# Second-half gates and two RG-LRU tiles moved ahead of the heads, five pairs of projection columns by seven block products

## The chip, the cores and the metric

The kernel runs on one core of one Trainium2 chip. The time is the device time of one execution in microseconds (us). Lower is better. TensorE (PE) does the matrix products, VectorE (DVE) and ScalarE (ACT) the elementwise work, GpSimd (POOL) a few copies, and the queue of SyncE (SP) issues nearly all transfers between HBM and the on-chip memory.

## The reference, cut to what matters

One layer of a hybrid decoder for 2048 prompt tokens and 8 sample rows, width 1024. Cut to the parts that the change touches:

```python
hn = _rmsnorm(x, g_norm) * (1.0 + scale[:, None]) + shift[:, None]
z = hn @ w_in                                  # 1024 x 5136
xa, za, q, k, v, glr, zg = jnp.split(z, SPLITS, axis=-1)
xc = conv_b + sum(xp[:, j:j + T] * conv_w[j] for j in range(CONV_W))
gx, ga = sigmoid(blockdiag(xc, w_gate_x)), sigmoid(blockdiag(xc, w_gate_a))
_, h = lax.associative_scan(_lin_comb, (a, u), axis=1)     # RG-LRU, a and u from gx, ga, xc
y_lru = h * silu(za)
o, S_new = _gla_chunked(qh, kh, vh, log_alpha, S0)         # 4 heads
y_gla = rmsnorm_per_head(o) * silu(zg)
mix = concat([y_lru, y_gla]) @ w_out                       # 2048 x 1024
x = x + gate[:, None] * mix                                # then a final RMSNorm
```

## The kernel before, in words

Every float32 product is made of three products of rounded parts: a matrix is split into a high part (a rounding copy on ACT) and a low part (a subtraction on DVE), and high*high, high*low and low*high are added in one PSUM bank. `hh` and `hl` are the two parts of the normalized input `hn` for 1024 tokens, transposed: eight blocks of 128 rows (`kt`) by 1024 tokens, with 8 more columns for the samples.

The tokens are worked off in two halves. The first half has 1024 tokens in two segments of 512. The second half has 1024 tokens and the 8 samples, 1032 columns in segments of 384, 384 and 264 (`SEGS`). `project` (L636 on, matmuls L642 to L644) makes one column tile of 128 output features for one segment: 24 matmuls.

In each half the loop over `HEADS` calls `gla_head`, then `lru`. A head computes its values (`values`, L327 to L329), q and k, its decay, and two tiles of its gate `zg` (`silu2`, L1031 and L1032); the chunked attention of 128 tokens at a time (`chunks`) is put between these units. `lru` does one to three of the eight RG-LRU tiles: `xa_unit` (projection, convolution, block-diagonal gates, scan at L1199) and `za_unit`. Tiles 6 and 7 of the second half are done after all heads, while the last part is prepared. The last part, the output projection (class `Pair`, matmuls at L1483), already uses seven block products in place of eight.

Order is set by hand with a clock. `after(u, f)` puts `f` into a heap with the due time clock + u, and `tick` moves the clock on by 1 for each projected segment, by 0.5 for each of the eight token tiles of `values`, and calls what is due. A call made during a tick counts its own `after` from the clock of that tick, so a chain with steps of 0.5 moves by one link per projected segment. The compiler's scheduler may then still reorder instructions that don't depend on each other; `behind(q)` pins an instruction behind the last one written so far on its engine.

One such chain is `out_weights`. It prepares the weights of the output projection in 16 steps `s`: 0 to 7 for one half of the output columns, 8 to 15 for the other; within each eight, four steps for the weights `wd[0]`, needed first, then four for `wd[1]`. A step loads `r` (L745, two transfers of 256 KB), multiplies it by the gate (two L766, 512 wide), makes four sums (L766, 256 wide), in the `wd[1]` steps also splits two of them (L770 and L771), stores seven or five blocks of 128 KB (L784), two more from the splits (L775), and loads the next `r`. The pool `hp`, which holds all this, has one buffer for `r`. A step has four links of 0.5 (six in a `wd[1]` step), then 0.5 and 1 up to the stores, 1 up to the next load, 1.5 up to the next first link. A pause (`phase`) holds the chain during the change of halves.

After the second half the pools `gp` (the heads) and `hp` are closed, and the pool `mp` is laid over their memory (`reuse_waits="tile"`: a tile of the new pool waits until the old tiles under it are done with). `load_w(0, 0, 0)` (L1347) then loads the first weights of the output projection into it, and `split_w` splits them (L1333 and L1336).

Of the kernel before, what the change touches and what calls it, by code (L numbers as in the profile page):

```python
# [34 lines left out]
SEGS = (((0, 512), (512, 512)), ((0, 384), (384, 384), (768, 264)))  # L35
HEADS = (3, 0, 1, 2)
LRU_TILES = ((0,), (1, 2), (3, 4), (5, 6, 7))

# [11 lines left out]
def hybrid_kernel(ctx, tc, i, o):  # L50
# [21 lines left out]

# [107 lines left out]
    def modulate(xt, g, kts):  # L180

        c = slice(g * 256, (g + 1) * 256)
        for k2 in range(kts[0], kts[1], 2):
            pt = tps().rearrange("p (k t) -> p k t", k=2)
            f = xp.tile([P, 2, 256], F32, tag="f512", name="hnf")
# [47 lines left out]
    def hn_load(g, now=True):  # L233

        xt = []
        for j in range(2):
            q = 2 * g + j
            if q in (0, 1, 7):
                x = xp.tile([P, TH + NS], F32, tag="xt", name="xt")[:, :D]
            elif q == 2:  # L240
                x = gp.tile([P, D], F32, tag="on", name="xo")
            else:
                x = gp.tile([P, D], F32, tag="vh" if q < 5 else "vl", name="xv", bufs=2)
# [386 lines left out]
    def open_lp():  # L630
# [3 lines left out]
        hp = hpx.enter_context(tc.tile_pool(name="hp", bufs=1, reuse_waits="tile"))  # L634
# [35 lines left out]
    def after(units, fn, gla=False):  # L670
        clock[1] += 1
        heapq.heappush(pend, (clock[0] + units, clock[1], fn, gla))
# [17 lines left out]
    def ada_gate():  # L690
# [3 lines left out]
        def step(kt):  # L694
# [4 lines left out]
            def mm():  # L699
# [6 lines left out]
                else:  # L706
# [3 lines left out]
                    after(4, out_weights)  # L710
# [5 lines left out]
    phase = [0]  # L716

    def out_weights():


        def begin(q):
# [5 lines left out]
            r = load(8 * q)  # L727

            def add():
                with behind(V):  # L730
                    V.tensor_tensor(g, g, bt, op=OP.add)
                after(0.5, lambda: step(8 * q, r, g))
# [15 lines left out]
        def one(ops, end):  # L748


            if phase[0] == 1:
                after(0.5, lambda: one(ops, end))
                return
# [5 lines left out]
        def step(s, r, g):  # L759
# [19 lines left out]
            def store():  # L779
# [19 lines left out]
        begin(0)  # L799
# [43 lines left out]
    def new_values():  # L843
        return [[gp.tile([P, 4, DV], F32R, tag=tag, name=tag, bufs=2) for _ in range(2)] for tag in ("vh", "vl")]
# [181 lines left out]

    def silu2(w, c0, n):

        ps = project(w, c0, n)
        z = lp.tile([P, 512], F32, tag="zs", name="zs", bufs=4)[:, :n]  # L1030
        S.activation(z, ps, AF.Tanh, scale=0.5)  # L1031
        V.scalar_tensor_tensor(z, z, 1.0, ps, op0=OP.add, op1=OP.mult)  # L1032
# [16 lines left out]
    def gla_head(half, h, wv=None):  # L1049
# [8 lines left out]
        prep, zs, os_, state, wz = {}, {}, [None], [], []  # L1058

        def chunks(s, c):  # L1060

            nch = min(SEGS[half][s][1], TH - SEGS[half][s][0]) // P
            if c == 0:
                prep[s, "run"] = gla_start(half, h, s, prep[s])
                after(1.5 if half else 1, lambda: chunks(s, 1), True)
                return
            gla_chunk(half, h, s, c - 1, prep[s], prep[s, "run"], v)
            if c < nch:
                after(1, lambda: chunks(s, c + 1), True)
                return  # L1070
            gla_norm(nch, prep[s, "run"])
            after(2.5 if half else 1 if s + 1 < ns else 2, lambda: finish(s), True)
# [823 lines left out]
```

## Time and profile before

| what | value |
|---|---|
| median of 3 runs | 1453.5 us (1451.63 to 1454.32) |
| span of the profiled execution | 1451.9 us |
| PE busy | 1429.6 us, 98% of the span |
| DVE busy | 993.1 us, 68% |
| ACT busy | 670.7 us, 46% |
| moved | 268.53 MB, mean 185 GB/s |
| granted TensorE clock | 0.998 |

The page gives the execution's own time as its span. The median of the runs is 1.6 us above it. A busy PE is not a PE at its peak, since a matmul's time in the trace includes its way through the pipeline: the 128x512 matmuls of the output projection are 390 ns long in the table of groups and start 227 ns apart. So the distance between starts is what a matmul costs.

By its lines, the trace falls into a start (to about 70 us), the first half (to about 570 us), the second half (to about 1072 us, when the last gate unit of tile 5 ends), tiles 6 and 7 (to about 1127 us) and the output projection.

### The profile page before, as it was taken

The page shows a single profiled execution, that of the slowest core. Times are in us where ns is not written, and L with a number is a line of the kernel's source. Part 1 is how long each engine was busy: PE and PEld are TensorE (multiplying, and loading weights), DVE is VectorE, ACT ScalarE, POOL GpSimd, SP SyncE. Part 2 cuts the span into 40 slices and gives each one's busy share as a digit, 9 for nine tenths or more (in the row PEclk, how much of TensorE's full clock was granted, in tenths as well). Part 3 has the DMA queues.
Part 4 walks back from the last instruction along what each step waited for, and adds up shares of the span by engine and source line. Part 5 has one row for each costly group of instructions (what it writes and reads, how often), then busy time and mean ns, then how long its engine had stood idle before and what let it go on. Part 6 is the DMA issues. An engine that isn't in the chain of part 4 may idle for free.

```text
span 1451.9 us, 23133 instructions
## 1 busy us (share of the span) xinstructions
PE 1429.6 (98%) x8753; PEld 1269.0 (87%) x8753; DVE 993.1 (68%) x2390; ACT 670.7 (46%) x1214; POOL 28.4 (2%) x44
## 2 busy tenths in 40 slices
PE   7999999999999999999999999999999999999998
PEld 6888888888898888999999999999998887788886
DVE  5756555765765778567567656576678976688886
ACT  4643533652545477534533643446267522144332
POOL 1200000000000002000000000000000000000000
PEclk9999999999999999999999999999999999999999
DMA  9755554645555664335645544564552767694452
GB/s 333 263 178 174 186 170 146 202 147 174 182 174 192 204 212 163 95 130 177 210 138 165 178 141 162 180 200 135 179 197 90 282 226 270 231 355 140 137 168 113
DMA packets 173605, 268.53 MB, mean 185 GB/s; under 512 B 10482, under 2 KB 126866, under 8 KB 171053
## 3 DMA queue, kind: packets, MB, share of 16 engines
q1 hardware_dynamic: 141093, 250.00, 50.9%
q10 hardware_dynamic: 32048, 16.00, 3.7%
q8 instruction: 69, 1.13, 0.3%
q0 software_dynamic: 352, 1.05, 0.2%
q14 instruction: 43, 0.35, 0.1%
HBM read 168.55 MB, written 98.52 MB: 184 GB/s over the span
## 4 chain that ended last, share of the span: by engine, by line
PE 52%; issue 34%; DVE 5%; ACT 4%; DMA 4%; SPq 1%; POOL 0%; ACTq 0%; DVEq 0%; POOLq 0%
PE acc L1483 12%; PE tp L1483 9%; PE acc L642 6%; PE acc L643 6%; PE acc L644 6%; PE acc L327 2%; PE acc L328 2%; PE acc L329 2%; DMA wada<-in_w_ada_dram 1%; DMA w<-parts 1%; PE po L976 1%; DVE cv L1145 1%; PE pss L1691 1%; ACT L881 1%; PE tp L942 0%
## 5 line engine op out<-in xcount | busy, mean ns | idle before, releaser
L642 PE MATMUL acc<-hh,w 128*128 128x384 f32 (+2 forms) x1256 | 446.2, 355 | 3.6 <-DMA w<-parts 3.3
L643 PE MATMUL acc<-hl,w 128*128 128x384 f32 (+2 forms) x1256 | 434.9, 346 | 0.0
L644 PE MATMUL acc<-hh,w 128*128 128x384 f32 (+2 forms) x1256 | 434.0, 346 | 0.0
L642 PEld LDWEIGHTS acc<-hh,w 128*128 128x128 f32 x1256 | 235.9, 188 | 26.2 <-DVE xb L899 3.6
L643 PEld LDWEIGHTS acc<-hl,w 128*128 128x128 f32 x1256 | 236.1, 188 | 19.4 <-issue 0.4
L644 PEld LDWEIGHTS acc<-hh,w 128*128 128x128 f32 x1256 | 235.9, 188 | 19.5
L1483 PE MATMUL acc<-w,a 128*128 128x512 f32 (+1 forms) x792 | 184.8, 386 | 0.0
L1483 PEld LDWEIGHTS acc<-w,a 128*128 128x128 f32 x792 | 146.8, 188 | 33.2 <-issue 3.4
L327 PE MATMUL acc<-w,hh 128*128 128x256 f32 (+1 forms) x508 | 145.5, 286 | 0.0
L329 PE MATMUL acc<-w,hl 128*128 128x256 f32 (+1 forms) x508 | 143.3, 282 | 0.2 <-DVE hl L216 0.2
L328 PE MATMUL acc<-w,hh 128*128 128x256 f32 (+1 forms) x508 | 143.1, 282 | 0.0
L1483 PE MATMUL tp<-w,a 128*128 128x512 f32 x564 | 136.0, 391 | 0.0
L1483 PEld LDWEIGHTS tp<-w,a 128*128 128x128 f32 x564 | 105.2, 188 | 26.8 <-issue 5.2
L1031 ACT ACTIVATE zs<-acc 128x512 f32<-128x512 f32 (+2 forms) x80 | 41.0, 513 | 177.3 <-PE acc L644 177.1
L1032 DVE SCALAR_TENSOR_TENSOR zs<-zs,acc 128x512 f32<-128x512 f32 (+2 forms) x80 | 46.2, 578 | 86.0 <-ACT zs L1031 81.4
L327 PEld LDWEIGHTS acc<-w,hh 128*128 128x128 f32 x508 | 96.0, 189 | 1.6 <-DVE vl L860 0.4
L329 PEld LDWEIGHTS acc<-w,hl 128*128 128x128 f32 x508 | 96.0, 189 | 0.4 <-DVE hl L216 0.4
L328 PEld LDWEIGHTS acc<-w,hh 128*128 128x128 f32 x508 | 95.5, 188 | 0.2
L1333 ACT CAST a<-s 128x512 fp32r<-128x512 f32 x61 | 36.5, 619 | 95.3 <-issue 35.9
L1145 DVE SCALAR_TENSOR_TENSOR cv<-xa,vecT,cv 128x512 f32<-128x512 f32 (+2 forms) x120 | 75.9, 640 | 1.8 <-ACT cv L1143 1.4
L158 ACT ACTIVATE junk<-on 128x256 bf16<-128x256 f32 x64 | 26.6, 416 | 78.0 <-DVE on L981 69.6
L859 ACT CAST vh<-acc 128x256 fp32r<-128x256 f32 x56 | 20.7, 370 | 90.0 <-PE acc L329 71.7
(343 smaller groups left out, 2234.6 us busy)
## 6 DMA issues: line engine op xcount, KB each, us to landing
w<-parts SPq DMA_DIRECT2D x38, 1024.0 KB
parts<-w SPq DMA_DIRECT2D x37, 1024.0 KB
wr<-in_w_in_dram SPq DMA_DIRECT2D x44, 512.0 KB
a<-mixd SPq DMA_DIRECT2D x63, 256.0 KB
w<-wd SPq DMA_DIRECT2D x12, 1024.0 KB
wada<-in_w_ada_dram SPq DMA_DIRECT2D x16, 512.0 KB
r<-in_w_out_dram SPq DMA_DIRECT2D x32, 256.0 KB
mixd<-zs ACTq DMA_DIRECT2D x32, 256.0 KB
```

The costliest lines, as they stand in the source:

```text
L158: S.activation(junk[:m, :n], x, AF.Square, accum_out=out)
L327: PE.matmul(ps, hh[:, kt, c], hi[:, kt % 4], start=kt == 0, stop=False)
L328: PE.matmul(ps, hh[:, kt, c], lo[:, kt % 4], start=False, stop=False)
L329: PE.matmul(ps, hl[:, kt, c], hi[:, kt % 4], start=False, stop=kt == KT - 1)
L642: PE.matmul(ps[:, :n], hi[:, kt], a, start=kt == 0, stop=False)
L643: PE.matmul(ps[:, :n], hi[:, kt], b, start=False, stop=False)
L644: PE.matmul(ps[:, :n], lo[:, kt], a, start=False, stop=kt == KT - 1)
L1031: S.activation(z, ps, AF.Tanh, scale=0.5)
L1032: V.scalar_tensor_tensor(z, z, 1.0, ps, op0=OP.add, op1=OP.mult)
L1145: V.scalar_tensor_tensor(cv[:, cq], xa[:, cq.start + k:cq.stop + k], cw[k], cv[:, cq], op0=OP.mult, op1=OP.add)
L1333: S.copy(t[:, 0, k], (low(t) if src is None else src)[:, k])
L1483: PE.matmul(ps, t[:, u, k], w[:, v, k, c], start=(q < 3 or ps is own) and (k, u, v) == (0, 0, 0), stop=(k, u) == (3, 1), skip_group_check= ...
```

## The change

The samples' columns of 12 column tiles (the eight gate tiles and the two RG-LRU tiles 0 and 1 with two projections each) move into the first half, whose second segment becomes 256 and 264 wide there (`SAMPLES`). In the second half these tiles then have 1024 columns, and they are done before all heads: the first head's two gate tiles by plain projections (`gates_ahead`), the others as five pairs of column tiles by `seven`. A pair's weights are a 2 by 2 block matrix (two halves of 512 rows, two column tiles), `hn` is one too (two halves of rows, 512 tokens twice), and seven block products of 12 matmuls, 512 wide, give what eight give now.

The block sums of `hn` (`sums`) are made once, on DVE and ACT, and lie in a pool `sp` on the memory of `gp` and `hp`; one block of `hn` is overwritten and restored afterwards (`a21d`). The sums and splits of the weights (`pair_weights`) are made in the first half, in a chain before `out_weights`, and stored in HBM (`twd`). `out_weights` starts only when both the gate and the five pairs are ready, is stopped at a step's end before tile 6 of the first half, and goes on when `sp` is closed. Steps that are left when the heads are done are worked off in one go (`while outw["busy"]`). Finished gates are kept in HBM (`zgd`) and loaded by each head. The heads then run with one RG-LRU tile each (2, 3, 4, 5).

```diff
+SAMPLES = ((0, 512), (512, 256), (768, 264))
+EARLY = (0, 1)
+LATE_TILES = ((2,), (3,), (4,), (5, 6, 7))
+PACE = ((1, 1), (1, 0.75, 1.5))
...
-                    after(4, out_weights)
+                    after(4, lambda: ready("gate"))
...
+    def pair_weights(n=0):
+        cols = zpairs()
+        if n == len(cols):
+            ready("pairs")
+            return
+        r = hp.tile([P, 2, KT, P], F32, tag="tr", name="tr")
+        for a, col in enumerate(cols[n]):
+            SP.dma_start(r[:, a], i["w_in"][0, :, col:col + P].rearrange("(k p) n -> p k n", p=P))
+        b11, b21, b12, b22 = r[:, 0, :4], r[:, 0, 4:], r[:, 1, :4], r[:, 1, 4:]
...
+        def split(k, x):
+            def f():
+                t = hp.tile([P, 4, P], F32R, tag="th", name="th", bufs=2)
+                S.copy(t, x)
+                V.tensor_tensor(x, x, t.bitcast(F32), op=OP.subtract)
+                def store():
+                    for u, y in enumerate((t.bitcast(F32), x)):
+                        SP.dma_start(twd[n, k, :, u], y.rearrange("p k n -> p (k n)"))
+                after(0.5, store)
+            return f
+        def one(ops):
+            if not ops:
+                after(1, lambda: pair_weights(n + 1))
+                return
+            with behind(V):
+                for f in ops[0]:
+                    f()
+            after(0.5, lambda: one(ops[1:]))
+        after(1.5, lambda: one([[sub(b11, b12, b11), sub(b12, b22, b12)], [sub(b22, b22, b11), sub(b21, b21, b22)]]
+                               + [[split(k, x)] for k, x in enumerate((b11, b22, b12, b21))]))
...
-                if s % 8 < 7:
+                if outw["stop"] or s == 15:
+                    outw["busy"], outw["next"] = False, s + 1
+                elif s % 8 < 7:
                     after(1, lambda: again(s + 1, g))
                 elif q == 0:
-                    after(1, lambda: begin(1))
+                    after(1, lambda: begin(s + 1))
...
+    def close_sp():
+        spx.close()
+        gp = gpx.enter_context(tc.tile_pool(name="gp", bufs=1, side="right", reuse_waits="tile"))
+        hp = hpx.enter_context(tc.tile_pool(name="hp", bufs=1, reuse_waits="tile"))
+        if outw["next"] < 16:
+            outw["stop"] = False
+            after(4, lambda: out_weights(outw["next"]))
...
+    def product(ps, q, n, start):
...
+        for k in range(4):
+            for u, v in ((0, 0), (0, 1), (1, 0)):
+                PE.matmul(ps, w[:, u, k], x[v][k], start=start and (k, u, v) == (0, 0, 0),
+                          stop=(k, u) == (3, 1), skip_group_check=True)
+            if k % 2:
+                drip()
+        tick(0.5)
...
+        x, e = acc(), None
+        product(x, ZB11, n, True)
+        y = acc()
+        S.copy(y, x)
...
+        e = acc()
+        product(e, ZT1, n, True)
+        es = xp.tile([P, 512], F32, tag="f512", name="es")
+        S.copy(es, e)
+        e = es
+        product(y, ZT2, n, False)
+        c = c2(0)
+        add(c, y, e)
+        f = acc()
+        product(f, ZB22, n, True)
+        add(c, c, f)
+        use(1, 0, c)
+        product(y, ZT3, n, False)
+        c = c2(1)
+        add(c, y, e)
+        use(1, 1, c)
...
         gla_head(0, h, wv0 if k == 0 else None)
         if k == 0:
             ada_gate()
+            pair_weights()
...
-    after(5, lambda: phase.__setitem__(0, 2))
+    gates_ahead(HEADS[0])
+    gates_seven(0)
+    for n in range(2):
+        lru_seven(n)
+        gates_seven(1 + n)
+    while drips:
+        drip()
+    for u, x in enumerate(a21()):
+        SP.dma_start(x.bitcast(F32), a21d[u])
+    close_sp()
     for k, h in enumerate(HEADS):
         gla_head(1, h)
-        lru(1, LRU_TILES[k][:1] if k == 3 else LRU_TILES[k])
+        lru(1, LATE_TILES[k][:1])
     flush_gla()
+    while outw["busy"]:
+        heapq.heappop(pend)[2]()
     gpx.close()
     hpx.close()
```

More of the change, by code (lines that the diff above doesn't have):

```diff
@@ L731, in add @@
                     V.tensor_tensor(g, g, bt, op=OP.add)
[L732 removed]
+                after(0.5, lambda: step(s, r, g))
             after(4, add)
@@ L1100, in gla_head @@
                 pk = None
-            if s == 0 and half == 1:
-                both = wp.tile([P, 2, 1088], F32R, tag="w", name="w", bufs=3)
-                with behind(S):
-                    S.copy(both[:1, 0, :1], ident[:1, :1])
-                wz.append(weights(ZG + 2 * h * P, P, both=both))
             if s + 1 < ns:
```

313 lines of the change are left out of this document (250 added, 63 removed).

## The prediction

> **What bounds the kernel now.** I read the page first, then the busy time by stage, then single starts on PE, then the transfer queue's waits and the chain near the end.
>
> ```profile
> span 1451.9 us, 23133 instructions
> ...
> PE 1429.6 (98%) x8753; PEld 1269.0 (87%) x8753; DVE 993.1 (68%) x2390; ACT 670.7 (46%) x1214; POOL 28.4 (2%) x44
> ```
>
> ```profile
> 70.00:520.00 450.00, 449.97 (x2497) 387.07 (x2496) 280.77 (x638) 206.21 (x338) 0.47 (x1) 1.00 0.55 177
> 520.00:575.00 55.00, 53.92 (x335) 45.04 (x334) 46.84 (x100) 39.97 (x67) 6.28 (x10) 1.00 0.60 197
> 575.00:1063.00 488.00, 483.97 (x3525) 471.80 (x3523) 315.76 (x991) 222.23 (x451) 4.05 (x7) 1.00 0.49 160
> 1063.00:1127.00 64.00, 62.06 (x394) 60.16 (x393) 47.63 (x92) 44.58 (x72) 2.40 (x3) 1.00 0.40 135
> 1127.00:1452.00 325.00, 317.63 (x1432) 253.51 (x1430) 255.06 (x424) 119.42 (x224) 2.77 (x4) 1.00 0.60 215
> ```
>
> The columns are stage, its length, then the busy time of PE, weight loads, DVE, ACT and POOL, the clock, the DMA share and GB/s. PE has work in every stage and idles 4 us of the 488 us of the second half. The clock is full. So each matmul taken away is worth its distance to the next start, as long as nothing else comes last. DVE is the next engine: 62%, 85%, 65%, 74% and 78% of the five stages. What is left of PE's waits is of this kind:
>
> ```profile
> 853.68 0.41 PE L642 MATMUL acc<-hh,w 128*128 128x384 f32 x1 [1.49 <-DMA w<-parts]
> ```
>
> ```profile
> 705.10 3.95 DMA wd<-t
> ...
> 709.55 6.42 DMA w<-parts
> ```
>
> The queue of SP is in order: at 705 us a store of `out_weights` stands in front of the next column's weights, and PE waits for these. This matters below.
>
> **The change, part by part.** Prices of matmuls, from starts in the timeline and a run of 48 in the chain of waits:
>
> ```profile
> 1137.79 10.88 PE acc L1483 x48
> ```
>
> ```profile
> 608.73 0.34 PE L642 MATMUL acc<-hh,w 128*128 128x384 f32 x1
> ...
> 612.89 0.53 PE L942 MATMUL tp<-xb,e 128*128 128x128 f32 x3
> ```
>
> ```profile
> 1069.57 0.28 PE L642 MATMUL acc<-hh,w 128*128 128x264 f32 x1
> ...
> 1072.45 0.34 PE L642 MATMUL acc<-hh,w 128*128 128x384 f32 x1
> ```
>
> ```profile
> 688.16 0.39 PE L327 MATMUL acc<-w,hh 128*128 128x256 f32 x1
> ...
> 710.04 0.34 PE L873 MATMUL acc<-gls,g2s 128*128 128x384 f32 x1
> ```
>
> A 512-wide matmul costs 10.88/48 = 0.2267 us, so 24 cost 5.44. From the next rows, 24 of 384 cost 4.16, 24 of 264 cost 2.88, and 192 of 256 cost 21.88, so 24 cost 2.74.
>
> Removed: 12 column tiles in the second half, each 4.16 + 4.16 + 2.88 = 11.20, together 134.4 us. Added there: the first head's two tiles at 2 x 5.44, 21.8, and five pairs of 84 matmuls at 0.2267, 95.2. Added in the first half: 12 tiles at 5.44 + 2.74 + 2.88 instead of 10.88, that is 0.18 each, 2.2. **PE's own sum is 21.8 + 95.2 + 2.2 - 134.4 = -15.2 us.** The gates of tiles 0 and 1 change by under 0.3, with both signs; nothing.
>
> Rows for what the other engines get:
>
> ```profile
> L292 DVE TENSOR_TENSOR w<-wr,w 128x1024 fp32r<-128x1024 f32 x37 | 45.1, 1219 | 6.9 <-ACT w L291 6.7
> L766 DVE TENSOR_TENSOR r<-r,g 128x512 f32<-128x512 f32 x32 | 21.9, 683 | 0.0
> L1032 DVE SCALAR_TENSOR_TENSOR zs<-zs,acc 128x384 f32<-128x384 f32 x32 | 17.6, 549 | 31.1 <-ACT zs L1031 26.5 <-DMA w<-wd 4.6
> L766 DVE TENSOR_TENSOR t<-r 128x256 f32<-128x256 f32 x32 | 13.4, 418 | 0.1
> L771 DVE TENSOR_TENSOR p<-t,p 128x256 fp32r<-128x256 f32 x8 | 3.3, 418 | 0.1
> ```
>
> ```profile
> L1497 ACT COPY p<-acc 128x512 f32<-128x512 f32 x16 | 9.4, 586 | 53.0 <-PE acc L1483 53.0
> L770 ACT CAST p<-t 128x256 fp32r<-128x256 f32 x8 | 3.3, 407 | 9.7 <-DVE t L766 9.7
> ```
>
> *Weights of the pairs.* Eight 512-wide DVE operations a pair, 40 x 0.68 = 27 us on DVE, 20 ACT copies of 0.59, 10 loads and 40 stores on SP. PE covers them: DVE goes from 281 to 308 of 450 us. Between 0 and +3 (a store in front of a weight load, as in the row at 853.68); I take 0, since the first half has no such row now.
>
> *Sums of hn.* 16 DVE operations of 1.22, 20 us, beside two projected segments of each gate tile and three products, about 19 us of PE. *The seven products.* A pair needs two ACT copies and three DVE sums, 3.2 us, of 19 us; its weights come in 512 KB pieces, one per 2.72 us, 193 GB/s, where the second half moved 160 and the last stage 215. The block restored and the first head's weights meet at the end. Below: 0. Above: 35 pieces at 160 GB/s take 115 us, +20. I take +3, nearer to the last stage, which moves as much beside the same kind of products.
>
> *Heads with less beside them.* The second half loses 8 gate tiles from DVE (1.5 us each by L1032) and two RG-LRU tiles (about 15 each: four operations of 1024 columns at 1.2 or more, some 18 of one segment at about 0.5), 42 us; PE loses 134. DVE then has 274 of some 354 us, 77% instead of 65%. The 78% of the last stage go with 7.4 idle us of PE in 325. Between 0 and +8; I take +2.
>
> *The chain `out_weights`.* This decides. It now starts after the pairs. In units of the clock, from head 0 to the stop before tile 6 there are 6 + 12 + 10 + 12 + 8 + 12 + 4 = 64 (tiles, heads by turns). A pair's links come due at whole ticks, 8 to 9 units (fewer in `values`); five take 40. The remaining 24, less 4.5 to begin, hold two to three steps of 7 to 10 units, and a step begun is ended: three. The second half has 4 x (4 + 6) + 4 x 6 = 64 units, less 8.5 to resume: six steps and the beginning of a seventh. So the rest of step 9 and **six whole steps, 10 to 15, are left** for the loop behind the heads. Before, the second half had 100 units, and:
>
> ```profile
> 542.03 1.32 SPq L745 DMA_DIRECT2D r<-in_w_out_dram  x2
> ```
>
> ```profile
> 1009.43 0.56 SPq L745 DMA_DIRECT2D r<-in_w_out_dram  x1
> ...
> 1012.08 0.55 SPq L745 DMA_DIRECT2D r<-in_w_out_dram  x1
> ```
>
> ```profile
> 1060.13 3.19 SPq L775 DMA_DIRECT2D wd<-p  x2
> 1064.84 0.32 SPq L1347 DMA_DIRECT2D w<-wd  x1
> ```
>
> Step 6 loads at 542 and step 15 at 1009 to 1012: nine steps in 468 us, some 10 units each with the pause; the last just ended with the heads. And who waited for it:
>
> ```profile
> SPq L1347 <- DMA wd<-p: 1.3, 1, 1.3
> ```
>
> ```profile
> 1063.00 1.73 DMA wd<-p
> ...
> 1065.21 6.73 DMA a<-mixd
> ...
> 1092.93 4.81 DVE w L1336 x8
> ```
>
> The first weight load of the output projection waited for the chain's very last store, although that store writes other weights (`wd2`): the new pool lies on `hp`. So all six steps come before the first product of the last stage, not only those that write its operand.
>
> A step in one go: the load of `r` lies between 1.73 (128 KB) and 6.42 us (1 MB), I take 3.5; DVE 2 x 0.68 + 4 x 0.42 = 3.0; stores between 1.73 and 3.95, I take 3.0, with one buffer for `r` before the next load. That is 9.5; with a split (0.41 + 0.42) 10.4. Two of the first and four of the second: 60.6.
>
> ```profile
> 1081.80 2.34 DVE L1199 TENSOR_TENSOR_SCAN tg<-xl,hc,tx 128x1024 f32<-128x1024 f32 x1
> ```
>
> ```profile
> 1126.71 0.86 PE L1483 MATMUL acc<-w,a 128*128 128x512 f32 x3
> ```
>
> Tile 5 leaves PE at 1072.4 and its scan ends at 1084.1. The loop's first operations are pinned behind what DVE was given before it, so they start about 12 us after tile 5. With 4 for the rest of step 9, 60.6, the weight load (6.5) and the first of eight splits (0.6 + 0.6), the first product stands 84 us behind tile 5. Before it stood at 1126.7, 54 us behind, and tiles 6 and 7 fill no more than that. **+30 us.** With the lower ends (no pinning, steps of 6.5 and 7.3) it is 53: 0. With the upper ends (13.4 and 14.2) 109: +55.
>
> [...]
>
> **Sum:** -15.2 + 3 + 2 + 30 = +20 on a span of 1451.9. The span is 1.6 us below the median of the runs, so against the median 1453.5 + 20, **1473 us**.
>
> **The rivals.** *The chain is hidden after all*: the compiler's scheduler lets the loop begin early, or the weights' place is free. Then -15.2 + 3 + 2: 1443, faster. For it: the lower ends give 53 against 54 us, and SP loads run ahead (the load at 542 stands before the pause's end). It decides where the last wd2 store lands less than 46 us behind tile 5. Against: `behind` and the one buffer of `r`. *The pieces of the seven come late*: +20 by the rate above instead of +3, with the chain hidden 1453.5 - 15.2 + 20 + 2 = 1460, slower; against it stand 215 GB/s at 60% share in the last stage. *DVE gets the upper hand in chain and heads*: 22 us of the chain's DVE work fall onto 64 us that have 48, and steps go to the upper ends: -15.2 + 3 + 8 + 45, 1494. *Nothing changes*, chain and gain cancelling: first product 65 to 72 us behind tile 5.
>
> **How the numbers follow.** Forecast (1460 to 1485) 0.55; DVE or later 0.12; late pieces without the chain 0.05; cancelled 0.05; hidden 0.23. About 0.2% (2.9 us) is what this kernel's runs can tell from no change. Slower 0.72, same 0.04, faster 0.24. The range, 1441 to 1495, leaves out one in ten on each side: a fully hidden chain with nothing lost elsewhere, and steps beyond the upper ends.
>
> **What would show it.** 420 matmuls in the 35 products, 227 ns apart, 95 us together; if longer, see whether operand loads (`w<-twd`) or DVE end the waits. The second half from its first head to tile 5 should be some 355 us. Stores of L784 should come in a row, about 10 us a step, after tile 5's end, with PE idle some 30 us before its first L1483. If the stores end earlier, or PE starts L1483 within 55 us of tile 5, the step on the chain is wrong, and the time is near 1443. If fewer than five `r` loads follow the last head, my count of units is wrong.

## The result and the profile after

The changed kernel is slower: 1522.5 us median (1517.4 to 1526.5, four runs) against 1453.9 us for the kernel before, a ratio of 1.047 with a 95% interval of 1.0447 to 1.0493. The prediction had the direction right (slower, 0.72) and the size wrong: 1473 us was forecast, and the result lies above the upper end of the range, 1495. The profiled execution of the changed kernel took 1517.4 us with a span of 1515.6 us, 63.7 us more than the span before; it is the fastest of the four, 5 us under the median.

The first rows of the page of the changed kernel:

```profile
span 1515.6 us, 23410 instructions
PE 1429.4 (94%) x8693; PEld 1249.2 (82%) x8693; DVE 1052.1 (69%) x2471; ACT 692.4 (46%) x1253; POOL 30.1 (2%) x44
PEclk9999999999999999999999999999956999999999
```

PE is busy as long as before (1429.6 us), but its share fell from 98% to 94%, and the clock row has two slices of 40 at 5 and 6 tenths. The busy times by stage of the changed kernel say where (stage, its length, PE, weight loads, DVE, ACT, POOL, clock, DMA share, GB/s):

```profile
70.00:520.00 450.00, 449.41 (x2770) 398.95 (x2769) 298.58 (x706) 214.42 (x376) 0.65 (x1) 1.00 0.61 197
520.00:600.00 80.00, 78.91 (x373) 63.82 (x372) 60.19 (x109) 59.50 (x92) 12.00 (x16) 1.00 0.45 163
600.00:709.00 109.00, 105.60 (x453) 83.84 (x451) 61.49 (x80) 43.31 (x58) 0.00 (x0) 1.00 0.67 223
709.00:1075.00 366.00, 358.18 (x2761) 343.85 (x2760) 258.30 (x861) 173.15 (x365) 0.00 (x0) 1.00 0.58 189
1075.00:1190.00 115.00, 55.82 (x328) 52.64 (x327) 70.40 (x150) 44.46 (x75) 2.41 (x3) 0.73 0.51 165
1190.00:1515.00 325.00, 318.42 (x1438) 254.25 (x1436) 256.22 (x426) 119.61 (x224) 2.78 (x4) 1.00 0.61 215
```

The stages are the first half, the change of halves with the first head's gates, the seven products, the heads, tiles 6 and 7, and the output projection. Only the fifth has a PE that idles for long: 59 of 115 us, at a granted clock of 0.73. That stage took 54 us before. The wait is one, in the table of PE's waits of the changed kernel (total, times, longest):

```profile
PE acc L1275 <- ACT xh L1255: 57.1, 1, 57.1
PE acc L335 <- DVE zs L1097: 4.0, 1, 4.0
```

From the starts in the traces I set four marks: the first and last of the seven products, the first matmul of the heads' values in the second half, the end of tile 5's projections, and the first matmul of the output projection. The difference of the last two is called the tail. All runs of this study, in us; each ratio is to runs of the kernel before that were taken together with that kernel, with medians of 1453.5 to 1453.9:

| kernel | seven products | heads begin | tile 5 ends | heads | output projection begins | tail | median | ratio to before, 95% interval |
|---|---|---|---|---|---|---|---|---|
| before | none | 566.9 | 1072.5 | 505.6 | 1126.7 | 54.3 | 1453.9 | |
| changed | 599.6 to 708.9 | 710.3 | 1075.2 | 364.9 | 1190.5 | 115.3 | 1522.5 | 1.0470 (1.0447 to 1.0493) |
| dense chain | 604.3 to 713.8 | 715.2 | 1094.8 | 379.6 | 1151.4 | 56.6 | 1479.4 | 1.0187 (1.0161 to 1.0214) |
| unpinned copy | 598.8 to 707.7 | 709.1 | 1078.2 | 369.1 | 1164.2 | 86.1 | 1502.0 | 1.0323 (1.0295 to 1.0352) |
| both | 602.6 to 712.1 | 713.4 | 1096.5 | 383.0 | 1153.7 | 57.2 | 1480.7 | 1.0183 (1.0167 to 1.0198) |
| resident operands | 599.9 to 708.7 | 710.1 | 1080.0 | 369.9 | 1195.7 | 115.7 | 1523.9 | 1.0482 (1.0462 to 1.0502) |
| early gates | 599.7 to 709.3 | 710.2 | 1085.4 | 375.1 | 1201.0 | 115.7 | 1527.7 | 1.0504 (1.0488 to 1.0519) |
| dense, stores on POOL | 603.4 to 713.0 | 714.4 | 1103.0 | 388.6 | 1159.9 | 56.9 | 1486.6 | 1.0222 (1.0207 to 1.0237) |
| that, unpinned, early gates | 603.5 to 712.9 | 713.8 | 1101.0 | 387.2 | 1157.7 | 56.7 | 1489.9 | 1.0241 (1.0217 to 1.0265) |
| that, dense in the heads only | 599.7 to 708.9 | 709.8 | 1103.3 | 393.5 | 1168.3 | 64.9 | 1497.5 | 1.0301 (1.0284 to 1.0318) |
| free buffer | 600.2 to 709.2 | 710.6 | 1081.2 | 370.6 | 1196.4 | 115.2 | 1521.7 | 1.0466 (1.0432 to 1.0499) |
| dense, unpinned, three queues | 604.6 to 714.6 | 717.0 | 1099.8 | 382.8 | 1158.0 | 58.2 | 1478.9 | 1.0177 (1.0142 to 1.0212) |
| that with the free buffer | 603.8 to 712.8 | 714.8 | 1087.9 | 373.2 | 1146.0 | 58.1 | 1474.2 | 1.0131 (1.0095 to 1.0167) |
| that, dense in the heads only | 599.5 to 708.5 | 710.9 | 1084.0 | 373.1 | 1151.3 | 67.3 | 1479.5 | 1.0171 (1.0140 to 1.0202) |

The stage times are those of one profiled execution each. The heads of the changed kernel took 364.9 us there and 369 to 370 us in the runs that have the same work in that stage (unpinned copy, resident operands), so a difference of 5 us in that column alone says little. Nor is the profiled execution always a typical one: that of "dense, unpinned, three queues" took 1485.3 us, 6.4 above its median, and that of "unpinned copy" 1495.6, 6.4 below.

### The profile page after: what moved, and what is told of

Same layout as the page of the kernel before. It is cut to its first block, busy times and chain, and to the rows that moved or that the text cites. A ratio compares the mean times of both kernels' runs of the same rounds, so it can differ in the third digit from the quotient of the medians.

```text
span 1515.6 us, 23410 instructions
## 1 busy us (share of the span) xinstructions
PE 1429.4 (94%) x8693; PEld 1249.2 (82%) x8693; DVE 1052.1 (69%) x2471; ACT 692.4 (46%) x1253; POOL 30.1 (2%) x44
## 4 chain that ended last, share of the span: by engine, by line
PE 78%; DVE 8%; ACT 5%; DMA 5%; issue 2%; SPq 1%; POOL 0%; DVEq 0%; ACTq 0%; POOLq 0%
PE acc L1792 12%; PE acc L650 10%; PE acc L652 10%; PE acc L651 10%; PE tp L1792 8%; PE acc L1514 5%; PE acc L335 4%; PE acc L336 4%; PE acc L337 4%; PE po L1044 1%; DMA r<-in_w_out_dram 1%; PE tp L1130 1%; DVE tg L1294 1%; PE tp L1010 1%; PE acc L1275 1%
## 5 line engine op out<-in xcount | busy, mean ns | idle before, releaser
L650 PE MATMUL acc<-hh,w 128*128 128x512 f32 (+3 forms) x1096 | 383.4, 350 | 1.8 <-DMA w<-parts 1.5
L651 PE MATMUL acc<-hl,w 128*128 128x512 f32 (+3 forms) x1096 | 372.9, 340 | 0.7 <-DVE hl L202 0.6
L652 PE MATMUL acc<-hh,w 128*128 128x512 f32 (+3 forms) x1096 | 372.5, 340 | 0.0
L650 PEld LDWEIGHTS acc<-hh,w 128*128 128x128 f32 x1096 | 206.2, 188 | 20.9 <-DVE f L973 1.8
L651 PEld LDWEIGHTS acc<-hl,w 128*128 128x128 f32 x1096 | 206.3, 188 | 19.0 <-DVE hl L202 1.9
L652 PEld LDWEIGHTS acc<-hh,w 128*128 128x128 f32 x1096 | 206.1, 188 | 17.4 <-issue 0.4
L1096 ACT ACTIVATE zs<-acc 128x512 f32<-128x512 f32 (+3 forms) x73 | 36.8, 505 | 119.9 <-PE acc L652 104.4
L1275 PE MATMUL acc<-xh,wg 128*128 128x512 f32 (+3 forms) x80 | 31.2, 392 | 57.8 <-ACT xh L1255 57.1
L1642 ACT CAST a<-s 128x512 fp32r<-128x512 f32 x61 | 36.5, 619 | 95.8 <-issue 36.2
L1097 DVE SCALAR_TENSOR_TENSOR zs<-zs,acc 128x512 f32<-128x512 f32 (+3 forms) x73 | 41.5, 568 | 51.4 <-ACT zs L1096 51.4
L1275 PEld LDWEIGHTS acc<-xh,wg 128*128 128x128 f32 x80 | 15.6, 197 | 63.7 <-ACT xh L1255 57.4
```

Source lines behind the costliest of these rows:

```text
L650: PE.matmul(ps[:, :n], hi[:, kt], a, start=kt == 0, stop=False)
L651: PE.matmul(ps[:, :n], hi[:, kt], b, start=False, stop=False)
L652: PE.matmul(ps[:, :n], lo[:, kt], a, start=False, stop=kt == KT - 1)
L1275: PE.matmul(ps, wgh[:, g], xh[:, c], start=True, stop=False)
```

## The tail: three runs on the chain

Where the 57 us come from is told by ACT's timeline in the changed kernel:

```profile
1096.56 0.48 ACT L1354 COPY xa<-acc 128x384 f32<-128x384 f32 x1 [2.04 <-PE acc L652]
1115.62 0.41 ACT L831 CAST p<-r 128x256 fp32r<-128x256 f32 x1 [18.58 <-DVE r L827]
...
1142.25 0.40 ACT L831 CAST p<-t 128x256 fp32r<-128x256 f32 x1 [1.44 <-DVE t L827]
1150.84 1.14 ACT L1642 CAST w<-w 128x512 fp32r<-128x512 f32 x2 [8.18 <-DMA w<-wd]
1152.55 0.62 ACT L1642 CAST a<-a 128x512 fp32r<-128x512 f32 x1 [0.57 <-DMA a<-mixd]
1153.07 0.51 ACT L1255 CAST xh<-cv 128x384 fp32r<-128x384 f32 x1
```

The last row is the rounding copy of tile 6's convolution (L1255), whose input had been ready for over 50 us (without this order, in a run below, it is done at 1093.5). It stands on ACT behind the chain's casts (L831) and behind the first splits of the output projection (L1642), and these wait for a weight load that waits for the chain's last store:

```profile
1095.82 1.21 SPq L809 DMA_DIRECT2D r<-in_w_out_dram  x2
...
1135.45 1.21 SPq L809 DMA_DIRECT2D r<-in_w_out_dram  x2
...
1142.24 1.87 SPq L836 DMA_DIRECT2D wd<-p  x4
1145.73 0.32 SPq L1656 DMA_DIRECT2D w<-wd  x1
```

These are rows of the transfer queue's timeline of the changed kernel. Six loads of `r` follow tile 5, at 1095.8 to 1135.5, and the weight load comes 3.5 us after the last stores are begun. The waits of that queue from 1140 to 1150 us name the stores (`wd<-p`) as what the weight load (L1656) waits for:

```profile
SPq L1656 <- DMA wd<-p: 1.4, 2, 0.9
```

The copy is written with `behind(S)` in the tiles of the last group, so it may not pass what ACT was given before it. After 1153 the rest of tiles 6 and 7 still takes PE 37 us (1153.6 to 1190.5). The theory after the result was therefore: the tail is the chain and the rest of the tiles one after the other, not the longer of the two. Three runs test it: take the left-over chain away, take the order away, take both.

**The chain made denser**, so that all sixteen steps are done before tile 5 ends:

```diff
-            one([[op(r[:, 0], r[:, 0], g, OP.mult)], [op(r[:, 1], r[:, 1], g, OP.mult)],
-                 [op(t[:, 1], b22, b12, OP.subtract), op(b12, b12, b11, OP.subtract)],
-                 [op(t[:, 0], b22, b12, OP.subtract), op(t[:, 2], b21, t[:, 0], OP.subtract)]]
-                + ([[lambda: split(0, b22)], [lambda: split(1, t[:, 2])]] if f else []), lambda: after(1, store))
+            one([[op(r[:, 0], r[:, 0], g, OP.mult), op(r[:, 1], r[:, 1], g, OP.mult)],
+                 [op(t[:, 1], b22, b12, OP.subtract), op(b12, b12, b11, OP.subtract),
+                  op(t[:, 0], b22, b12, OP.subtract), op(t[:, 2], b21, t[:, 0], OP.subtract)]]
+                + ([[lambda: split(0, b22), lambda: split(1, t[:, 2])]] if f else []), store)
...
-            after(1.5, lambda: step(s, r, g))
+            after(1, lambda: step(s, r, g))
```

> The links of the chain that prepares the output projection's weights are put closer together (two links per step in place of four, the store and the next first link sooner), so that by my count no step is left when the heads are done. Theory A (the 62 us lost behind tile 5 are the six left-over steps and nothing else): the first product stands about 55 us behind tile 5 as before the change, and the time falls by about 60 us to 1462 us (1455 to 1470); the denser chain may cost PE a few us in the heads. Rival B (the seven block products and the heads lose the time, the chain only stands where PE would wait anyway): it stays above 1500.

Measured: 1479.4 us, no load of `r` behind tile 5, and a tail of 56.6 us, within 2.3 us of the tail before. So 58.7 of the tail's 61 us hang on the left-over chain. The whole time was expected lower, near 1462: the heads took 15 us more than in the changed kernel, which the section on the heads takes up.

**The order taken away**: the rounding copy of tiles 6 and 7 (and of tile 7 in the first half, which has the same line) is no longer put behind ACT's earlier work.

```diff
             def split():
-                with behind(S):
-                    S.copy(xh[:, c], cv[:, c])
+                S.copy(xh[:, c], cv[:, c])
```

> The rounding copies of tiles 6 and 7 are no longer pinned behind the last ScalarE instruction written before them; the six left-over steps stay. Theory A1 (tiles 6 and 7 cannot cover the chain because their rounding copies stand on ScalarE behind the first split of the output projection's operands, which waits for the chain): PE works on tiles 6 and 7 during the chain, the first product stands about 71 + 14 = 85 us behind tile 5 in place of 116, and the time falls by about 30 us to 1492 us (1483 to 1500). Rival A2 (the chain's own instructions hold VectorE or its memory holds the loads of tiles 6 and 7, whatever the pins): no change, 1517 to 1527.

Measured: 1502.0 us, tail 86.1 us, with the six steps still behind tile 5. PE's longest wait is now another, as the table of waits of this run shows (its lines are one smaller from here on, so L1791 is the output projection):

```profile
PE acc L1791 <- ACT a L1641: 23.1, 1, 23.1
```

Tiles 6 and 7 now run beside the chain and end first, and PE waits 23 us for the first operand of the output projection. Of the 61 us, 29 are lost only where the order of the copy meets a left-over chain (115.3 - 86.1), and the other 32 belong to the chain as such.

**Both.**

> Both edits. If nothing is left of the chain, the pin has nothing to wait for: the same as the dense chain alone within 5 us, about 1460 us. If some steps are still left in the dense chain, this one is faster than it by up to their 8 us each.

Measured: 1480.7 us and a tail of 57.2 us, as with the dense chain alone. Where nothing is left over, the order of the copy costs nothing.

## The seven products: are the operands late?

The stage of the seven products is 109.3 us long and the 420 matmuls are 95.2; the last products of the first head's gates (10) and the gate products of tiles 0 and 1 (24) fill some 8 of the difference, and about 6 us are stalls. Late operands were a rival in the prediction. In this run only the first six operand tiles are loaded, and the other products take these again, so it leaves out 29 loads, and its output is not that of the layer.

```diff
+        if len(kept) == 6:
+            place = kept.pop(0)
+            kept.append(place)
+            return place
         if operands:
...
-        return w.rearrange("p u (k n) -> p u k n", k=4)
+        kept.append(w.rearrange("p u (k n) -> p u k n", k=4))
+        return kept[-1]
```

> Only the first six weight operands of the seven block products are loaded; the later 29 products use these again, so the output is not the reference's: it leaves out 29 loads of 512 KB. The products' stage loses 8.8 us against the distances of its matmuls. Theory S1 (operands come late): the time falls by 5 to 9 us, to about 1515 us. Rival S2 (PE waits for sums, PSUM places and silus on VectorE and ScalarE): it falls by under 2 us, 1520 to 1523 us.

Measured: 1523.9 us, the stage from 599.9 to 708.7, 108.8 us. The busy times of that run for the stage have the DMA share at 0.25 instead of 0.67 and PE's busy time where it was:

```profile
600.00:708.70 108.70, 106.07 (x454) 84.19 (x453) 61.75 (x81) 43.69 (x58) 0.00 (x0) 1.00 0.25 85
```

Late operands fall. What is left are PSUM places, block sums and silus, and the changed kernel's waits in that stage name them for 3.4 us:

```profile
PE acc L1514 <- ACT acc L1528: 1.3, 2, 0.7
PE acc L1514 <- ACT gs L1535: 1.2, 1, 1.2
PE acc L1514 <- DVE zs L1097: 0.9, 2, 0.6
```

## The heads: one wait, one queue, and a clock

With the tail settled, the dense chain's 1479 us still lie 26 us above the kernel before, though PE has 15 us less work. The other runs look for the rest.

The 4.0 us wait at the start of the heads is longer than it looks. These rows are PE's timeline of the dense run around a wait of the same kind, for a head's weights:

```profile
932.91 0.34 PE L652 MATMUL acc<-hh,w 128*128 128x384 f32 x1
938.46 0.66 PE L650 MATMUL acc<-hh,w 128*128 128x384 f32 x1 [5.20 <-DMA w<-parts]
938.91 0.52 PE L651 MATMUL acc<-hl,w 128*128 128x384 f32 x1
939.23 0.52 PE L652 MATMUL acc<-hh,w 128*128 128x384 f32 x1
...
944.03 0.52 PE L652 MATMUL acc<-hh,w 128*128 128x384 f32 x1
944.35 0.47 PE L650 MATMUL acc<-hh,w 128*128 128x384 f32 x1
944.66 0.34 PE L651 MATMUL acc<-hl,w 128*128 128x384 f32 x1
944.83 0.33 PE L652 MATMUL acc<-hh,w 128*128 128x384 f32 x1
```

After the wait the matmuls start 0.32 us apart for 5.9 us and then 0.17 us again: the wait of 5.2 us costs another 2.7. The busy times of the dense run show the granted clock (the third number from the end) at a half in that stretch:

```profile
938.00:944.00 6.00, 5.54 (x17) 5.58 (x18) 0.00 (x0) 0.00 (x0) 0.00 (x0) 0.50 0.38 153
```

After a wait of 1.47 us in the changed kernel the matmuls start 0.17 to 0.18 us apart from the second on, and the granted clock is 1.00 from 830 to 860 us:

```profile
833.83 0.34 PE L652 MATMUL acc<-hh,w 128*128 128x384 f32 x1
835.64 0.41 PE L650 MATMUL acc<-hh,w 128*128 128x384 f32 x1 [1.47 <-DMA w<-parts]
835.89 0.34 PE L651 MATMUL acc<-hl,w 128*128 128x384 f32 x1
836.06 0.34 PE L652 MATMUL acc<-hh,w 128*128 128x384 f32 x1
```

So two things were tried: to remove the wait before the heads, and to remove the waits for weights.

**The gates of tiles 0 and 1 sooner**, on the theory that VectorE is still busy with tile 1 when the last silu should run:

```diff
-                after(3 if j == LRU_TILES[3][-1] or half == 1 and j != LRU_TILES[3][0] else 2, lambda: gates(t, [s]))
+                after(1.5 if seven else 3 if j == LRU_TILES[3][-1] or half == 1 and j != LRU_TILES[3][0] else 2, lambda: gates(t, [s]))
```

> One edit: in the pairs of column tiles the gate products of tiles 0 and 1 come 1.5 units of the heap's clock behind the convolution instead of 3, so three block products (some 8 us) sooner; the work is the same. Theory P (the one wait of TensorE between the seven products and the heads, 4.0 us at 711.78 in the changed kernel, comes from VectorE and ScalarE still working off tile 1's gates in order, so that the last pair's silu gives its PSUM place back late, and the matmuls behind it run 0.227 us apart instead of 0.125 for some 4 us): the wait falls to under 1.5 us, the slower matmuls are gone, from the first matmul of the heads' values to the end of tile 5 some 360 us instead of 366, the seven products within 1 us of 109.3. By this theory the six whole steps of the output weights still follow tile 5 and the tail stays 115 us, so the time is some 5 us under the changed kernel's. Rival Q (the place is freed late by ScalarE's own queue, whose stores of the gates wait for VectorE and for their buffers, wherever tile 1 stands): the wait stays 3 to 4 us and the time stays within 2 us of the changed kernel's. Rival R (gates asked for sooner wait for their own split): 2 to 5 us of new waits inside the seven products and no gain.

Measured: 1527.7 us, and the wait grew from 4.0 to 6.4 us. That theory falls. ACT's timeline of this run shows the other one:

```profile
704.68 1.29 ACTq L664 DMA_DIRECT2D mixd<-zs  x2
706.07 0.48 ACTq L1569 DMA_DIRECT2D zgd<-zs  x1
713.01 0.63 ACT L1096 ACTIVATE zs<-zs 128x512 f32<-128x512 f32 x1 [10.75 <-DMA mixd<-zs]
```

The next tanh (L1096) waits 10.75 us until stores issued at 704.7 have left one of the four `zs` buffers. By this row it is the buffers, and not the engines' work, that give the PSUM place back late; the next run tests it.

**A free buffer.** The two sums of the second and third gate pair go to a tile that is free after the block sums, so a pair needs four `zs` instead of six:

```diff
-        seven(n, use, lambda s: new_zs(), n == 0)
+        seven(n, use, lambda s: fs4[2][:, 2 * (n % 2) + s] if n else new_zs(), n == 0)
```

> One edit in the changed kernel: in the second and third pair of gate tiles the two sums C11 and C12 go to a buffer that lies free after the block sums, instead of to two of the four gate buffers; no work is added or left out. Theory Z (the wait of 4.0 us between the seven products and the heads comes from the four gate buffers: the last silus wait until the stores of the ones before have landed, and so give the PSUM places back late): the wait falls under 1.5 us and the matmuls behind it run 0.125 us apart at once; from the first matmul of the heads' values to the end of tile 5 some 360 us instead of 365, the time some 5 us under the changed kernel's (1510 to 1517, with the tail as it was). Rival Q (ScalarE's in-order queue alone: a store of gates that it issues waits for VectorE, and the next silu stands behind it): the wait stays between 3 and 7 us and the time where it was, 1517 to 1523.

Measured: 1521.7 us, no difference to the changed kernel. The wait did fall, in the waits of this run:

```profile
PE acc L650 <- DMA w<-parts: 3.6, 1, 3.6
...
PE acc L335 <- DVE zs L1097: 1.5, 1, 1.5
```

and the matmuls behind it run 0.125 us apart at once. But the wait for a weight tile near 833 us, 1.5 us in the changed kernel, is 3.6 us here, with matmuls 0.32 us apart behind it (starts at 837.47 and 837.79 us) and a granted clock of 0.94 from 830 to 860 us. The cause of the wait is shown; the gain of 5 us did not come. A wait further on took its place, but no run shows whether that is all of it.

**The queue.** In the dense run SP's queue has the stores of the chain and the loads of the stored gates ahead of a head's weights; its timeline before the 5.2 us wait:

```profile
921.64 0.80 SPq L1173 DMA_DIRECT2D zs<-zgd  x2
922.49 1.21 SPq L809 DMA_DIRECT2D r<-in_w_out_dram  x2
...
926.71 3.19 SPq L845 DMA_DIRECT2D wd<-r  x4
930.04 1.32 SPq L845 DMA_DIRECT2D wd<-t  x3
931.56 0.55 SPq L809 DMA_DIRECT2D r<-in_w_out_dram  x1
932.16 0.60 SPq L302 DMA_DIRECT2D w<-parts  x1
```

First the chain's stores alone were moved to POOL's queue (the two lines are L836 and L845):

```diff
-                        SP.dma_start(wd2[n, :, h, m, c], p[:, h].bitcast(F32))
+                        G.dma_start(wd2[n, :, h, m, c], p[:, h].bitcast(F32))
...
-                            SP.dma_start(wd[f, k, :, m, c], x[:, n])
+                            G.dma_start(wd[f, k, :, m, c], x[:, n])
```

> The dense chain of the first run (two links fewer per step, stores at once) with its stores of wd and wd2 issued from GpSimd's queue instead of SyncE's; loads stay where they were. In the dense run SyncE's queue stood 50.4 us in all for the stores of r, and TensorE waited 5.2 us for a head's weight tile whose load stood behind them, after which matmuls ran 0.32 us apart instead of 0.173 for 6 us. Theory Q1 (the order of SyncE's queue makes the heads slower when the chain is dense): the wait for a weight tile goes, the heads take 366 to 372 us instead of 380.7, time 1469 (1465 to 1474) against 1479. Rival D (VectorE, whose share rose, holds up the heads in many small places): the heads stay at 378 to 382 and the time within 2 us of 1479. Rival G (issuing from GpSimd takes longer per store, and the chain is longer for it): a step takes some 5 us more, one or two steps stay behind tile 5, 1480 or more.

Measured: 1486.6 us, a ratio of 1.0222 against 1.0187 of the dense chain. The queue's waits beside the heads tell why this was no test of the theory; first the dense run:

```profile
SPq L845 <- DVE r L827: 50.4, 10, 18.8
...
SPq L1173 <- DMA mixd<-zs: 33.7, 12, 10.1
```

and with the stores on POOL's queue:

```profile
SPq L1173 <- DMA mixd<-zs: 52.2, 15, 8.6
SPq L809 <- DMA wd<-r: 49.8, 7, 21.6
```

The wait changed its place: SP no longer stands at the stores, where it waited for VectorE's sums (50.4 us), but at the next load of `r`, still on SP, where it waits for those same stores (49.8 us), because `r` has one buffer. Two further kernels, one with the unpinned copy and the early gates as well, and one with the dense pace in the heads only, share the fault:

> Everything that the runs so far point to in one kernel: the dense chain, its stores on GpSimd's queue, the gates of tiles 0 and 1 sooner, and the rounding copy of tiles 6 and 7 not put behind the split of the output projection's operand. If the causes add up (theories P and Q1): heads 362 to 368 us, tail 55 to 58, first half and seven products as in the dense run (seven products from 604), time 1464 (1457 to 1470). If the heads are slower by the dense chain's VectorE work (rival D): 1473 to 1480. In both cases above the kernel before, whose 1453.6 would need the first half's 4 to 9 us and the 9 us of stalls in the seven products as well.

> As the run before, but the chain is dense only in the second half, beside the heads; in the first half it keeps the changed kernel's pace, so three steps are done there instead of six, and thirteen are left for the heads' 365 us. A dense step took some 31 us beside the heads, so ten to twelve fit and one to three are left behind tile 5, at some 7 us each. If the first half's extra 5 us in the dense run came from the dense chain: seven products from 599 to 600 instead of 604. Heads 365 to 372; the tail 56 to 62 with the unpinned copy covering what is left; time 1463 (1456 to 1472). If VectorE has no room for dense steps beside the heads (rival D): heads 380 or more, four or more steps left, 1485 or more.

Measured: 1489.9 and 1497.5 us. The second has the seven products at 599.7 again, so the 3 to 5 us that the dense kernels before it lose in the first half are the chain's own (three steps in place of six there), but its heads took 393.5 us. The tail is 64.9 us: the last of the thirteen steps loads its `r` at 1093, 10 us before tile 5 ends.

Then the chain's loads and the gates' loads were moved as well, so that SP holds none of the three:

```diff
-                SP.dma_start(r[:, a], i["w_out"][0, k * P:(k + 1) * P].rearrange("p (b n) -> p b n", b=2)[:, :, q * 256:q * 256 + 256])
+                G.dma_start(r[:, a], i["w_out"][0, k * P:(k + 1) * P].rearrange("p (b n) -> p b n", b=2)[:, :, q * 256:q * 256 + 256])
...
-                SP.dma_start(z[:, :n], zgd[2 * h + dt][:, c0:c0 + n])
+                G.dma_start(z[:, :n], zgd[2 * h + dt][:, c0:c0 + n])
```

> The third run (dense chain, unpinned copy) with three kinds of transfer moved off SyncE's queue to GpSimd's: the chain's loads of w_out, its stores, and the heads' loads of the stored gates. In the run that moved the stores alone, SyncE's queue stood 49.8 us for the loads of r, which wait for those stores, where it had stood 50.4 us for the stores: the wait had only changed its place, so that run did not test the queue. Theory Q1 (weight tiles come late because their loads stand behind the chain's transfers and the gate loads on SyncE's in-order queue): no wait of TensorE for a weight tile over 2 us beside the heads, heads 368 to 374 us instead of 384, time 1469 (1464 to 1474) against 1480.7. Rival D (VectorE holds the heads up): heads 380 or more, time within 3 us of 1480. Rival G (on GpSimd's queue the gates come late instead): new waits for the gates' output or four or more steps behind tile 5, 1483 or more.

Measured: 1478.9 us and heads of 382.8 us, the same as on SP's queue (1480.7 and 383.0). PE's waits in this run:

```profile
PE acc L650 <- DVE vl L928: 6.1, 1, 6.1
PE acc L650 <- DMA w<-parts: 4.6, 2, 3.4
PE acc L335 <- DVE zs L1097: 3.8, 1, 3.8
```

The waits for weights went from 10.1 us in all (longest 6.2) to 4.6 (longest 3.4), so the queue did delay them. But a wait of 6.1 us for VectorE (`vl`, the low part of a head's values) came in their place, and the median did not move beyond its interval. That the queue makes the heads slower is not borne out as a price of its own. The profiled execution lies 6.4 us above the median here, so its heads may be longer than usual.

> The run before with the two sums of the second and third gate pair in the free buffer as well. If theories Z and Q1 both hold, their gains add: heads 363 to 368 us, time 1464 (1459 to 1469). What then is left over the kernel before is the first half (4 to 9 us more, of which 2 are the transposes of the block sums), the 9 us of stalls inside the seven products and a tail longer by 2, against 15 us less of TensorE work. If Q1 falls and Z holds: 1475. If both fall: 1480.

Measured: 1474.2 us, heads 373.2 us. With the waits for weights already short, the medians differ by 4.7 us, about the 5 expected of the free buffer, and no new wait comes: the longest of PE in this run is 2.9 us. The heads of the two profiled executions differ by 9.6 us, but the other one is the execution 6.4 us above its median. This kernel is the fastest of the changed ones, though its interval overlaps that of the run before it, and it is still 1.3% slower (0.95% to 1.67%) than the kernel before the change. Of the 18.8 us between the spans (1470.7 and 1451.9), 15.4 lie ahead of tile 5's end. So with the tail settled, the 15 us that the seven products take off PE's work are still lost beside it: some 4 to the dense chain in the first half, 9 to stalls around the seven products, the rest spread over the first half and the heads. What exactly the dense chain costs the heads stays open.

> As the run before, with the dense chain in the second half only: three steps of the sixteen are done in the first half, thirteen are left for the heads. In the run of this kind with the loads on SyncE's queue the first half was 4 us shorter than with the dense chain in both halves, and SyncE's queue stood 105 us for the loads of r. Theory Q1: off that queue the steps take 27 to 30 us each, so one or none is left behind tile 5; heads 363 to 370 us, first half as in the changed kernel (seven products from 599 to 600), tail 56 to 60, time 1461 (1455 to 1468). Rival D (the steps are paced by the heap's clock and VectorE, not by the queue): three or more steps are left, tail 70 or more, 1475 or more.

Measured: 1479.5 us. The first half is short again (599.5), the heads are as before it (373.1), but thirteen steps at 31 us each reach past tile 5, and the tail is 67.3 us. Nothing is gained over the dense pace in both halves.

## Why the prediction was wrong, by its own steps

By the prediction's terms tile 5 should have ended at 1062.3 us (1072.5 - 134.4 + 21.8 + 95.2 + 2.2 + 3 + 2), and the tail should have been 84.3 us. Tile 5 ended at 1075.2, 12.9 us later, and the tail was 115.3 us, 31.0 longer. The output projection took 325.1 us, as before (325.2). The two differences, 43.9, are what lies between the forecast span of 1471.7 (1451.9 + 19.8) and the measured 1515.6. (From their own terms, the chain's lower and upper end in the prediction are 53.9 and 107.3 us, not 53 and 109; that changes no conclusion.)

**PE's own sum, -15.2: right as far as the trace can tell.** The products start 227 ns apart where nothing stalls. With every matmul priced at the usual distance of its shape, PE's work up to the end of tile 5 is about 14 us less than before, and the first half has 2.7 us more (2.2 counted). Tile 5 ended 2.8 us later than before, not 14 earlier, so about 17 us of new stalls stand against that gain, where the forecast had 5.

**Weights of the pairs, 0 (0 to +3): too low.** The second half begins 6.3 us later than before; 2.7 are products, and about 3.5 are many stalls, nearly all below 1 us. No run separated the pairs from the other work of that half, so what in it costs them stays open.

**Sums and seven products, +3 (0 to +20): +9.** About 9 us are stalls: some 6 in the seven products, the rest in the first head's gates. The upper end was built on late operands, and these are not the cause.

**Heads, +2 (0 to +8): +6.** The stage has about 6 us more of stalls than before, by the same prices. The step took DVE's share as the risk; the trace has instead one wait of 4.0 us for a PSUM place, held up by four buffers, and the slow matmuls behind it. DVE is at 258 of 366 us, 71%, where 77% was feared. The change also set the links of the chunks closer (`PACE`: 1, 0.75 and 1.5 units in place of 1.5, 1 and 2.5); no run separates that from the rest.

**The chain, +30 (0 to +55): +61, and this is the step that failed.** Its count was right to the step: three steps in the first half (loads of `r` at 351, 419 and 460), six whole ones left over. Its length was right too: the prediction has the first product 84 us behind tile 5, and in the trace ACT and PE get on with work 78 us behind it (1153.6 - 1075.2). Inside, the loop's first load comes 20.6 us behind tile 5 (12 and 4 were taken), and six steps take 49.9 us up to the weight load (60.6 were taken): a load of `r` is issued 7.5 to 7.6 us after the one before in the steps without a split and 8.1 to 8.3 with one, against 9.5 and 10.4. So two errors of the sum, a late start and short steps, partly cancel. In the run with the unpinned copy, where the tiles run beside the chain as the prediction had it, the loop starts 20.2 us behind tile 5 and the six steps take 58.8 us (1098.4 to 1157.2), close to the 60.6.

What failed is the sentence behind that number: "tiles 6 and 7 fill no more than that". It took the tail as the longer of chain and tiles, as if the two ran beside each other. The chain's 78 us contain only the 21 us of the tiles' projections that had been issued before PE stopped; the copy that the rest needs stood behind the split of the output operand on ACT, so 37 us of tiles came after the chain, the first 7 of them at half the clock (0.50 granted from 1153 to 1160 us). 78 + 37 = 115. The order was in the code of the kernel before as well, but the weight load ahead of the copy waited only 1.3 us there. The expected sign, PE idle ahead of its first product of the output projection, came at another place for the same reason: PE idles 57 us ahead of tile 6's gate products. Without the order, the tail is 86.1 us, close to the 84.3 predicted. That run's span is 1493.8 us, 22 above the forecast: tile 5 ends 15.9 us late, the tail is 1.8 longer and the output projection 4.4; its median lies another 8 above the span.

Of the rivals, "DVE gets the upper hand in chain and heads" (1494) came nearest to the time, but not by its mechanism (the steps were shorter than forecast, not longer), and "the pieces of the seven come late" was tested and fell.

## What to carry to other kernels

When work is left over at a seam, don't take the longer of two strands: follow, engine by engine, what is queued in order behind the one that waits, because an instruction that is pinned behind a waiting one turns "beside" into "after" (here 29 of the tail's 61 us). A transfer moved to another queue can leave its wait behind: with the chain's stores alone moved, SP stood 49.8 us at the loads of `r` where it had stood 50.4 at the stores. So read the waits of the old queue again before the run is called a test. Price a long wait of the matrix engine with the slow matmuls that may follow it: here the one of 5.2 us cost 2.7 more, and behind the one of 1.47 us there were none.

## What was not expected of the hardware

Matmuls ran at half the clock behind the longer gaps of PE. Between 75 and 1060 us, the traces of this study have 23 gaps of 3.4 to 7.2 us in PE's starts (beyond the usual distance), and behind each the granted clock is at a half for 3.4 or 6.8 us. The matmuls then start, for example, 0.32 us apart instead of 0.173 (384 columns) or 0.227 instead of 0.125 (272 columns). Of the gaps between 1.9 and 3.1 us, the clock falls to a half behind nine, one of them of 2.4 us (the dense chain with its stores on POOL's queue, at 928 us), and stays full behind the others; what decides there is not shown. The kernel before has no gap over 1.8 us in that stretch, and its clock is full there. So the wait of 4.0 us that begins at 712 us in the changed kernel cost nearly 6: it is followed by 3.4 us at a granted clock of 0.50 (716.5 to 719.9 us), with matmuls 0.227 us apart instead of 0.125.
